# A new order for the opening of an encoder step, with a third pair of projections run ahead

## The chip, the cores and the metric

The kernel runs on one core of a Trainium2 chip. The metric is the time of one execution on the device in microseconds (us); less is better. The engines are named as the profile names them: PE is TensorE's matmul, PEld its weight load, DVE VectorE, ACT ScalarE, POOL GpSimd, and SP SyncE, whose queue issues nearly all transfers.

## The reference

One layer of a streaming encoder works on 1024 prompt positions and 8 times 16 sample positions, 1152 rows (T) in all, in float32.

```python
h = rmsnorm(x, g_pre_mix)
qa, ka, va, qb, kb, vb, ga, gb = split(h @ w_in)          # 34 tiles of 128 columns
oa = band_attention(qa, ka, va, t5 bias, sink)             # 2 chunks back
ob = band_attention(qb, kb, vb, relative bias)             # 8 chunks back
x = x + rmsnorm((sigmoid(ga) * (oa @ w_oa) + sigmoid(gb) * (ob @ w_ob)) @ w_out, g_post_mix)
u, g = split(rmsnorm(x, g_pre_ffn) @ w_upg)
x = x + rmsnorm((gelu(causal_conv3(u)) * g) @ w_down, g_post_ffn)
```

It returns x and the new key, value and convolution rows. Only the first two lines and the two bias tables bear on this change.

## The kernel before

**Stage.** Everything that changes lies in the kernel's first stage: h is made and multiplied by `w_in`. Each float32 operand is kept as two float32r parts, a high one (a rounded copy that ACT makes) and a low one (the rest, that DVE makes by a subtraction), and a product takes three matmuls, high by high, low by high, high by low.

**Pairs and the seven products.** Two 128-column tiles of `w_in` form a pair (`pairs`, line 199; twelve of them). The 1024 features and the 1152 rows are each cut in two, and a pair is computed by a scheme of seven block products in place of eight, on sums and differences of blocks. The right factors are b11, b21 (first 576 rows, two halves of the features), b12, b22 (last 576 rows) and four sums t1 to t4. The 576 rows of a half are done in two chunks of 256 and 320 columns, so a block product is 24 matmuls (`product`, `chunk_product`, lines 137 to 148).

**What is run ahead.** Two of a pair's products, a11 by b11 and a12 by b21, need only the first 576 rows and no sums. For the first `NA` = 7 pairs they are done before everything else by the class `Away` (line 234): it splits two weight tiles into parts (`ih`, line 176 ACT and 177 DVE), `run(i, c)` does 12 matmuls of product i on chunk c (`ixh`), and `copy(i, c)` takes the running sum out of PSUM (`ia0h`, `ia1h`, line 251); run(1, c) adds to the same bank and so waits for copy(0, c). The results are stored (lines 253, 255) and loaded again later (`ia`, line 483).

**The opening.** The 1152 rows come as nine blocks of 128 (`xt`). A block goes through five steps: `enter` (ACT squares and sums, line 296, then DVE line 96 and POOL line 97 make the inverse root), `norm` (DVE, line 306, or 303 for blocks 0 and 1), `transposed` (PE, eight transposes into two PSUM banks, line 314), `high` (ACT copies out of PSUM, line 330) and `low` (DVE, line 335; only the rows of b11 and b21, blocks 0 to 3 and half of 4). Chunk 0 of b11 and b21 is blocks 0 and 1; chunk 1 is blocks 2, 3 and half of 4. Blocks 4 (second half) to 8 fill b12 and b22. A list written by hand (lines 345 to 405) gives the order of these steps and of the Away steps of pairs 0 and 1 on ACT, DVE and PE; each of these engines takes what it is given strictly in order. Pair 2's Away comes behind the list, then those of pairs 3 to 6 (line 511).

**The tables of biases.** In the opening the two tables are made (`eb`, lines 410 to 415; `ea`, lines 417 to 424, by one small matmul `pe`), stored to DRAM (`tab_b`, `tab_a`) and spread there by `replicate` (line 87) to 128 copies for each of eight heads: `ext_b` and `ext_a`, eight transfers each on SP. The attention stage reads them from about 287 us on.

**The tails.** `right_factors` (line 429) makes t3, t2, t1, the parts of b22, t4 and the parts of b12, one step for each `next(forms)`. Then `tail` (line 486) does the pairs one after the other: for a pair that was run ahead five products (t3 into `iz`, then t2, t1, b22 into `ix`, then t4 into `iz`), 120 matmuls. Between them `take` (line 487, DVE line 191) adds the stored part `ia` to the running sum, before PE may add the next product to the same bank. Weights come by `weights(f)` (line 217, two transfers `iw`, two buffers shared with those of Away), the left sums by `left_factors` (lines 127 to 133). Tail 0 is that of pair 0, and so on.

**What sets the order elsewhere.** Behind the list a scheduler orders each engine's instructions at build time: those written first go first among those that it believes ready. SP's queue is one line in that order. `issue_after(x)` puts what it holds behind x on x's own engine.

Of the kernel before, what the change touches and what calls it, by code (L numbers as in the profile page):

```python
# [14 lines left out]
ALU = mybir.AluOpType  # L15
# [37 lines left out]
def encoder_step(ctx, tc, x, w_in, w_o, w_out, w_upg, w_down, kc, vc, state_conv, conv_w, conv_b,  # L53
# [30 lines left out]
        return [[(r1[2 * g + i] if g < 2 else r2).tile([P, KD, GW], F32R, name=f"{name}{g}{'hl'[i]}", tag="act")  # L84
                 for i in range(2)] for g in range(NG)]

    def replicate(tab, ext, sb, n):

        nc.sync.dma_start(tab[:], sb[:])
        t = tab[:]  # L90
        for h in range(8):
            nc.sync.dma_start(ext[h], bass.AP(tensor=t.tensor, offset=t.offset + h * n, ap=[[0, P], [1, n]]))
# [57 lines left out]
    def banks(pool, name, widths=(CW, CW)):  # L150
        return [pool.tile([P, 512], F32, name=f"{name}_{c}", tag="ps")[:, 0:n] for c, n in enumerate(widths)]
# [6 lines left out]
    def chunk(c):  # L158
        return slice(c * widths[0], widths[0] + c * widths[1])
# [3 lines left out]
    with ExitStack() as ph:  # L163
# [7 lines left out]

        b12, b22 = [rq.tile([P, 4, 2 * CW], F32, name=n) for n in ("b12", "b22")]

        def split_left(src, name):
            sp = wop.tile([P, 2, 4, P], F32R, name=name, tag="wop")
            nc.scalar.activation(sp[:, 0], src, AF.Copy)  # L176
            nc.vector.tensor_tensor(sp[:, 1], src, fr(sp[:, 0]), op=ALU.subtract)
            return sp

        def two_chunks(name):  # L180
            return pa.tile([P, 2 * CW], F32, name=name, tag="a")

        def copy_out(ps, t):
            for c in range(2):
# [3 lines left out]
        def plus(ps, t, out=None):  # L188
# [2 lines left out]
                nc.vector.tensor_tensor(out[:, chunk(c)], ps[c], t[:, chunk(c)], op=ALU.add)  # L191
            return out

        def store(t, tile_no, half):
            nc.sync.dma_start(in_dr[tile_no][:, half * 2 * CW:(half + 1) * 2 * CW], t[:])

# [15 lines left out]
        def weights(f):  # L214
            raw = wraw.tile([P, 2, KD, P], F32, name=f"iw{f}", tag="uw")
            for i in range(2):
                nc.sync.dma_start(raw[:, i], w_in[pairs[f][i]])
            return raw
# [15 lines left out]
        class Away:  # L234


            def __init__(self, f, pool, early=False):
                self.f, self.pool, self.early = f, pool, early
                raw = away_weights(f)
                self.left = [split_left(raw[:, 4 * i:4 * i + 4], f"ih1{i}_{f}") for i in range(2)]  # L240
                self.out = [two_chunks(f"ia{i}h{f}") for i in range(2)]
                self.ps = [None, None]

            def run(self, i, c):
# [19 lines left out]
        with ExitStack() as pre:  # L264
# [70 lines left out]
                            nc.vector.tensor_tensor(xk[q][:, 1, :, t], pt[:, :, c], fr(xk[q][:, 0, :, t]),  # L335
                                                    op=ALU.subtract)

            b = []

            def enter():  # L340
                b.append(Block(len(b)))
                b[-1].square()

            with tc.manual_schedule(engines={mybir.EngineType.Activation, mybir.EngineType.DVE, mybir.EngineType.PE}):
                enter()
                b[0].norm()
                enter()
                b[0].transposed()
                for i in range(2):
                    nc.scalar.activation(gp[:, i * 512:(i + 1) * 512], gps[i][:], AF.Copy)  # L350
                b[1].norm()
                b[0].high()
                b[0].low()
                w0 = Away(0, psx, True)
                b[1].transposed()
                b[1].high()
                b[1].low()
                enter()
                w0.run(0, 0)
                b[2].norm()  # L360
                w0.copy(0, 0)
                w1 = Away(1, psx, True)
                enter()
                b[2].transposed()
                b[2].high()
                w0.run(1, 0)
                b[2].low()
                b[3].norm()
                w0.copy(1, 0)
                enter()  # L370
                w1.run(0, 0)
                b[3].transposed()
                b[3].high()
                b[4].norm()
                w1.copy(0, 0)
                b[3].low()
                w1.run(1, 0)
                b[4].transposed()
                b[4].high()
                b[4].low()  # L380
                w1.copy(1, 0)
                enter()
                b[5].norm()
                w0.run(0, 1)
                w0.copy(0, 1)
                enter()
                w1.run(0, 1)
                b[5].transposed()
                b[5].high()
                w1.copy(0, 1)  # L390
                b[6].norm()
                w0.run(1, 1)
                enter()
                w0.copy(1, 1)
                b[6].transposed()
                b[6].high()
                b[7].norm()
                w1.run(1, 1)
                enter()
                w1.copy(1, 1)  # L400
                b[7].transposed()
                b[7].high()
                b[8].norm()
                b[8].transposed()
                b[8].high()

            Away(2, psx).all()


            rr = xs.tile([8, 2 * CLIP + 1], F32, name="rr")  # L410
# [2 lines left out]
            nc.vector.memset(eb[:, 0:512], 0.0)  # L413
            nc.vector.tensor_scalar(eb[:, 0:512], eb[:, 0:512], rr[:, 0:1], -1.0, op0=ALU.add, op1=ALU.mult)
            nc.vector.tensor_scalar(eb[:, 512:EXT_B], rr[:, 0:EXT_B - 512], -1.0, None, op0=ALU.mult)
            replicate(tab_b, ext_b, eb, EXT_B)
            tt = xs.tile([T5_BUCKETS, 8], F32, name="tt")
            oh = xs.tile([T5_BUCKETS, EXT_A], F32, name="oh")
            nc.sync.dma_start(tt[:], t5t)
# [2 lines left out]
            nc.tensor.matmul(pe[0:8, 0:EXT_A], tt[:], oh[:], start=True, stop=True)  # L422
            ea = xs.tile([8, EXT_A], F32, name="ea")
            nc.scalar.activation(ea[:], pe[0:8, 0:EXT_A], AF.Copy, scale=-1.0)
            replicate(tab_a, ext_a, ea, EXT_A)

        tpool = [ph.enter_context(tc.tile_pool(name=f"t{i}", bufs=1, reuse_waits="tile")) for i in (3, 2, 1, 4)]

        def right_factors():

            for n, pool in zip(("t3", "t2", "t1"), tpool):
                rf[n] = pool.tile([P, 2, 4, 2 * CW], F32R, name=n)
            sums = tpool[3].tile([P, 2, 4, 2 * CW], F32, name="sums", tag="t")
            t3 = t2 = sums[:, 0]
            t1 = sums[:, 1]

            def sub(c, out, a, b):
                nc.vector.tensor_tensor(*[t[:, :, chunk(c)] for t in (out, a, b)], op=ALU.subtract)

            def part(name, i):  # L440
                return fr(rf[name][:, i])

            for c in range(2):
                sub(c, t3, b22, b12)
                parts_of(rf["t3"], c, t3)
            yield
            for c in range(2):
                sub(c, t1, b12, part("b11", 0))
                sub(c, t1, t1, part("b11", 1))
                sub(c, t2, b22, t1)  # L450
                parts_of(rf["t2"], c, t2)
            yield
            for c in range(2):
                parts_of(rf["t1"], c, t1)
            yield
            for c in range(2):
                parts_of(rf["b22"], c, b22)
            yield
            for c in range(2):
                sub(c, b22, part("b21", 0), t2)  # L460
                nc.vector.tensor_tensor(*[t[:, :, chunk(c)] for t in (b22, b22, part("b21", 1))], op=ALU.add)
            rf["t4"] = tpool[3].tile([P, 2, 4, 2 * CW], F32R, name="t4", tag="t")
            for c in range(2):
                parts_of(rf["t4"], c, b22)
            yield
            for c in range(2):
                parts_of(rf["b12"], c, b12)
            yield
# [12 lines left out]
        def head_back(f):  # L481
            a = two_chunks(f"ia{f}")
            nc.sync.dma_start(a[:], a1_dr[f][:])
            return left_factors(weights(f), True, f"i{f}", split_left), banks(psx, f"ix{f}", widths), a

        def tail(f, ops, xb, a, forms):
            def take(name):
                t = two_chunks(f"{name}{f}")
                return copy_out(xb, t) if a is None else plus(xb, a, t)

            t0, t1 = pairs[f]
            zb = banks(psz, f"iz{f}", widths)
            product(zb, next(ops), of(rf["t3"]), True, False)
            next(forms, None)
            product(xb, next(ops), of(rf["t2"]), a is not None, False)
            next(forms, None)
            u2 = take("iu")
            product(xb, next(ops), of(rf["t1"]), False, False)
            next(forms, None)
            u4 = take("iv")  # L500
            store(plus(zb, u4), t1, 1)
            product(xb, next(ops), of(rf["b22"]), False, True)
            next(forms, None)
            store(take("iw"), t0, 1)
            product(zb, next(ops), of(rf["t4"]), False, True)
            store(plus(zb, u2), t1, 0)
            next(forms, None)

        forms = right_factors()
        next(forms)  # L510
        for f in range(3, NA):
            Away(f, psz if f % 2 else psx).all()
        for f in range(len(pairs)):
            tail(f, *(head_back(f) if f < NA else head(f)), forms)


    wr = wr_stack.enter_context(tc.tile_pool(name="wr", bufs=2, side="right", reuse_waits="tile"))
# [1187 lines left out]
```

## Time and profile before

| | |
|---|---|
| time, median of 3 runs | 1612.9 us (1612.63 to 1615.28) |
| the profiled execution's own time | 1616.09 us |
| its span in the trace | 1614.3 us |
| PE busy | 1587.8 us (98%) |
| DVE busy | 1106.3 us (69%) |
| ACT busy | 727.7 us (45%) |
| granted clock of PE | 0.997 of full speed |

The profiled execution took 1.8 us more than its span, which is what lies around the traced instructions. Matmuls overlap, and their ends are modelled, so PE counts as busy also where it runs thin: in the opening the number of matmuls done in a stretch tells more than the busy time. In rows of the timeline the first number is the start, the second the length of the whole row; the time in brackets is how long the engine had been idle before it, and the name behind the arrow what ended that. A wait on several things is put down to the last one by the profile, which can name an engine that had long been done.

### The profile page before, as it was taken

The page shows a single profiled execution, that of the slowest core. Times are in us where ns is not written, and L with a number is a line of the kernel's source. Part 1 is how long each engine was busy: PE and PEld are TensorE (multiplying, and loading weights), DVE is VectorE, ACT ScalarE, POOL GpSimd, SP SyncE. Part 2 cuts the span into 40 slices and gives each one's busy share as a digit, 9 for nine tenths or more (in the row PEclk, how much of TensorE's full clock was granted, in tenths as well). Part 3 has the DMA queues.
Part 4 walks back from the last instruction along what each step waited for, and adds up shares of the span by engine and source line. Part 5 has one row for each costly group of instructions (what it writes and reads, how often), then busy time and mean ns, then how long its engine had stood idle before and what let it go on. Part 6 is the DMA issues. An engine that isn't in the chain of part 4 may idle for free.

```text
span 1614.3 us, 27934 instructions
## 1 busy us (share of the span) xinstructions
PE 1587.8 (98%) x10891; PEld 1467.1 (91%) x10891; DVE 1106.3 (69%) x2055; ACT 727.7 (45%) x1428; POOL 212.5 (13%) x287
## 2 busy tenths in 40 slices
PE   8999999999999999999999999999999999999998
PEld 7999999878788789988899999999999998888886
DVE  6976534677777765453498777667666677956987
ACT  7621233666555554332374444444444445434353
POOL 1000000221110004410002221122111211000002
PEclk9999999999999999999999999999999999999999
DMA  7654321754543164452253333212222128063023
GB/s 274 219 185 147 110 96 75 228 177 145 165 151 128 63 219 155 126 184 97 73 172 107 112 97 97 77 62 82 74 77 79 59 75 347 1 223 110 1 83 152
DMA packets 93045, 205.94 MB, mean 128 GB/s; under 512 B 19321, under 2 KB 42793, under 8 KB 92914
## 3 DMA queue, kind: packets, MB, share of 16 engines
q1 hardware_dynamic: 92640, 203.35, 36.7%
q8 instruction: 85, 1.39, 0.4%
q0 software_dynamic: 272, 0.81, 0.1%
q14 instruction: 46, 0.38, 0.1%
q10 hardware_dynamic: 2, 0.00, 0.0%
HBM read 147.61 MB, written 61.24 MB: 129 GB/s over the span
## 4 chain that ended last, share of the span: by engine, by line
PE 87%; DVE 4%; DMA 2%; ACT 2%; issue 1%; SPq 0%; DVEq 0%; POOLq 0%; ACTq 0%
PE x L143 18%; PE z L143 10%; PE x L1487 8%; PE ix L143 7%; PE p L1487 6%; PE iz L143 4%; PE y L143 4%; PE o L754 2%; PE d L117 2%; PE d L119 2%; PE pt L739 2%; PE d L118 2%; PE xh L143 2%; PE mp L965 2%; PE mp L967 2%; PE mp L966 2%
## 5 line engine op out<-in xcount | busy, mean ns | idle before, releaser
L143 PE MATMUL x<-xot,s 128*128 128x288 f32 x1152 | 157.7, 295 | 0.0
L143 PEld LDWEIGHTS x<-xot,s 128*128 128x128 f32 x1152 | 155.0, 188 | 0.1
L1487 PE MATMUL x<-wbp,zap 128*128 128x512 f32 x576 | 135.3, 389 | 0.0
L1487 PEld LDWEIGHTS x<-wbp,zap 128*128 128x128 f32 x576 | 108.1, 188 | 22.4
L705 ACT ACTIVATE p<-p,m 128x256 f32<-128x256 f32 (+4 forms) x128 | 74.8, 586 | 59.1 <-DVE m L700 59.0
L1487 PE MATMUL p<-wbp,zap 128*128 128x512 f32 x432 | 100.7, 389 | 0.1
L1088 ACT ACTIVATE s<-uw 128x512 fp32r<-128x512 f32 x96 | 60.2, 628 | 85.2 <-PE z L143 38.3
L1487 PEld LDWEIGHTS p<-wbp,zap 128*128 128x128 f32 x432 | 81.0, 188 | 17.3 <-ACT yacc L1497 0.5
L1292 DVE SCALAR_TENSOR_TENSOR wk<-w,cw,wk 128x448 f32<-128x448 f32 (+1 forms) x144 | 88.0, 651 | 2.8 <-ACT wk L1290 1.9
L1089 DVE TENSOR_TENSOR s<-uw,s 128x512 fp32r<-128x512 f32 x96 | 67.9, 708 | 31.1 <-ACT s L1088 30.7
L1089 DVE TENSOR_TENSOR a<-uw,a 128x512 fp32r<-128x512 f32 x62 | 42.8, 691 | 58.4 <-ACT a L1088 57.4
L143 PE MATMUL z<-xot,a 128*128 128x288 f32 x576 | 80.8, 295 | 0.0
L143 PE MATMUL x<-xob,s 128*128 128x288 f32 x576 | 80.8, 295 | 0.0
L143 PE MATMUL z<-xot,s 128*128 128x288 f32 x576 | 80.7, 295 | 0.0
L143 PEld LDWEIGHTS x<-xob,s 128*128 128x128 f32 x576 | 78.1, 188 | 0.1
L143 PEld LDWEIGHTS z<-xot,a 128*128 128x128 f32 x576 | 78.2, 188 | 0.0
L143 PE MATMUL ix<-t,s_i 128*128 128x256 f32 (+1 forms) x576 | 78.1, 294 | 0.0
L143 PEld LDWEIGHTS z<-xot,s 128*128 128x128 f32 x576 | 78.1, 188 | 0.0
L143 PEld LDWEIGHTS ix<-t,s_i 128*128 128x128 f32 x576 | 76.7, 188 | 0.0
L176 ACT ACTIVATE s_i<-iw 128x512 fp32r<-128x512 f32 x48 | 30.1, 631 | 83.8 <-PE ix L143 38.1
L143 PE MATMUL x<-xob,a 128*128 128x288 f32 x456 | 64.0, 295 | 0.0
L143 PE MATMUL y<-xob,a 128*128 128x288 f32 x456 | 64.0, 295 | 0.0
(638 smaller groups left out, 3832.6 us busy)
## 6 DMA issues: line engine op xcount, KB each, us to landing
uw<-in_w_upg SPq DMA_DIRECT2D x53, 512.0 KB, 3.8
iw<-in_w_in SPq DMA_DIRECT2D x24, 512.0 KB, 3.8
gg<-in_dr SPq DMA_DIRECT2D x16, 576.0 KB, 3.8
z_dr<-wk SPq DMA_DIRECT2D x23, 256.0 KB, 2.1
in_dr<-gt SPq DMA_DIRECT2D x30, 192.0 KB, 1.9
z_dr<-wk SPq DMA_DIRECT2D x23, 224.0 KB, 1.9
xt<-in_x SPq DMA_DIRECT2D x9, 512.0 KB, 7.8
oT<-o_dr SPq DMA_DIRECT2D x8, 576.0 KB, 4.3
```

What stands on the lines that cost most here:

```text
L117: nc.tensor.matmul(ps, w[:, 0, a], xg[0][:, b], start=start and k == 0, stop=False)
L118: nc.tensor.matmul(ps, w[:, 0, a], xg[1][:, b], start=False, stop=False)
L119: nc.tensor.matmul(ps, w[:, 1, a], xg[0][:, b], start=False, stop=stop and k == nk - 1)
L143: nc.tensor.matmul(ps, w[:, i, k], right(j, c, k), start=first and n == 0, stop=last and n == len(todo) - 1, skip_group_check=True)
L705: nc.scalar.activation(p[h][:, 0:n], p[h][:, 0:n], AF.Exp, bias=least[h], scale=-1.0, accum_out=st.d[:, h, i:i + 1])
L739: nc.tensor.transpose(pt[:, h * nb + b], st.p[i][h][:, c:c + P], ident[:])
L754: nc.tensor.matmul(ps[r, c], k.vs[:, kb, r], p[h], start=n == 0, stop=n == len(st.pv) - 1)
L965: nc.tensor.matmul(ps[:], self.sp[:, 0, k], oT[k][:, 0, c], start=k % 4 == 0, stop=False)
L1088: split["left"] = nc.scalar.activation(sp[:, 0], src, AF.Copy)
L1089: split["low"] = nc.vector.tensor_tensor(sp[:, 1], src, fr(sp[:, 0]), op=ALU.subtract)
L1292: nc.vector.scalar_tensor_tensor(out, src(t), cw[:, f, t:t + 1], out, op0=ALU.mult, op1=ALU.add)
L1487: nc.tensor.matmul(ps, z[:, i, k, c], w[:, j, k], start=first and n == 0, stop=last and n == 2, skip_group_check=True)
```

## The change

1. The list of the opening is written as a string of steps in another order. Pair 2's Away (`w.2`, `run.2.*`, `cp.2.*`) is now in the list, with its parts and outputs in pools of its own (`wop3`, `pa3`). `w.0` comes ahead of `transposed.0`, and block 8 and 7 come ahead of 5 and 6.
2. `replicate` keeps only the sixteen spreading transfers, and these are issued behind the last store of tail 2. The two small stores to `tab_b` and `tab_a` stay where they were.
3. The pools of t1 to t4 are opened in another order, 4 first, so that the scratch tile `sums` lies elsewhere in memory.
4. Tail 0 makes t2 before its own first left sum, which is put behind the last of t2's subtractions on DVE.
5. The weights of pairs 4 and 6 (for Away) are asked for with those of pair 3, and pair 0's full weights before Away 5 is run.

```diff
-    def replicate(tab, ext, sb, n):
-        nc.sync.dma_start(tab[:], sb[:])
+    def replicate(tab, ext, n):
...
-            with tc.manual_schedule(engines={...}):
-                enter()
-                b[0].norm()
-                enter()
-                b[0].transposed()
...
-            Away(2, psx).all()
+            wop3, pa3 = [pre.enter_context(tc.tile_pool(name=n, bufs=2)) for n in ("wop3", "pa3")]
+            def weights_of(f):
+                w[f] = Away(f, psx, True, wop if f < 2 else wop3, pa if f < 2 else pa3)
...
+                written = """
+                    enter.0 norm.0 enter.1 w.0 transposed.0 gp norm.1 high.0 transposed.1 low.0 enter.2 high.1 low.1
+                    run.0.0.0 norm.2 enter.3 w.1 norm.3 run.1.0.0 cp.0.0.0 enter.4 transposed.2 w.2 high.2 low.2
+                    transposed.3 run.2.0.0 norm.4 enter.8 run.0.1.0 high.3 cp.1.0.0 transposed.4 low.3 norm.8
+                    enter.7 high.4 low.4 cp.0.1.0 norm.7 run.1.1.0 transposed.8 enter.5 enter.6 norm.5 norm.6 high.8
+                    cp.1.1.0 run.0.0.1 transposed.7 cp.2.0.0 run.2.0.1 transposed.5 high.7 transposed.6 high.5
+                    run.1.0.1 high.6 run.2.1.0 cp.0.0.1 cp.1.0.1 run.0.1.1 run.1.1.1 cp.2.0.1 cp.1.1.1 run.2.1.1
+                    cp.2.1.0 cp.0.1.1 cp.2.1.1
+                """
...
-            replicate(tab_b, ext_b, eb, EXT_B)
+            nc.sync.dma_start(tab_b[:], eb[:])
...
-            replicate(tab_a, ext_a, ea, EXT_A)
+            nc.sync.dma_start(tab_a[:], ea[:])
...
-        tpool = [... for i in (3, 2, 1, 4)]
+        tpool = {i: ... for i in (4, 3, 2, 1)}
...
-            return left_factors(weights(f), True, f"i{f}", split_left), banks(psx, f"ix{f}", widths), a
+            raw = raws.pop(f, None) or weights(f)
+            return left_factors(raw, True, f"i{f}", split_left), banks(psx, f"ix{f}", widths), a
...
-            product(zb, next(ops), of(rf["t3"]), True, False)
-            next(forms, None)
+            if f:
+                first = next(ops)
+            else:
+                next(forms)
+                with tc.issue_after(rf["sub"].ins):
+                    first = next(ops)
+            product(zb, first, of(rf["t3"]), True, False)
...
         for f in range(3, NA):
-            Away(f, psz if f % 2 else psx).all()
+            e = Away(f, psz if f % 2 else psx)
+            if f == 3:
+                away_weights(4)
+                away_weights(6)
+            if f == 5:
+                raws[0] = weights(0)
+            e.all()
         for f in range(len(pairs)):
             tail(f, *(head_back(f) if f < NA else head(f)), forms)
+            if f == 2:
+                with tc.issue_after(held["store"].ins):
+                    replicate(tab_b, ext_b, EXT_B)
+                    replicate(tab_a, ext_a, EXT_A)
```

In the list `run.f.i.c` is run(i, c) of pair f, `cp.f.i.c` its copy, `w.f` the making of its parts, and the number behind the other names is the block.

## Rows read from the trace of the kernel before

**Rows 1.** The page, its first part (busy time of each engine with its share of the span and its instructions) and the head of its fourth (the chain of work that ended last, by engine).

```profile
PE 1587.8 (98%) x10891; PEld 1467.1 (91%) x10891; DVE 1106.3 (69%) x2055; ACT 727.7 (45%) x1428; POOL 212.5 (13%) x287
...
PE 87%; DVE 4%; DMA 2%; ACT 2%; issue 1%; SPq 0%; DVEq 0%; POOLq 0%; ACTq 0%
```

**Rows 2.** The timeline of PE, from the first product to the third tail: start, length, what, count of matmuls, idle before.

```profile
11.47 3.06 PE L143 MATMUL ixh<-xk,ih 128*128 128x256 f32 x12
...
24.40 1.04 PE L314 MATMUL tp<-ident,xn 128*128 128x128 f32 x8
...
44.33 0.81 PE L422 MATMUL pe<-oh,tt 32*8 32x384 f32 x2
45.06 15.11 PE L143 MATMUL ixh<-xk,ih 128*128 128x256 f32 x113
...
68.27 3.44 PE L143 MATMUL ixh<-xk,ih 128*128 128x256 f32 x24 [0.73 <-ACT ia0h L251]
71.55 3.33 PE L143 MATMUL iz<-t,s_i 128*128 128x256 f32 x24
...
85.98 2.92 PE L143 MATMUL iz<-t,a_i 128*128 128x256 f32 x20 [0.91 <-DVE a_i L177]
88.74 3.33 PE L143 MATMUL iz<-t,s_i 128*128 128x256 f32 x24
...
104.60 3.33 PE L143 MATMUL iz<-t,s_i 128*128 128x256 f32 x24
```

**Rows 3.** The stretches 20 to 30, 30 to 40 and 70 to 80 us: length, then busy time and count of PE, PEld, DVE, ACT, POOL, then granted clock, DMA share, GB/s.

```profile
20.00:30.00 10.00, 8.31 (x62) 7.61 (x61) 5.79 (x12) 7.37 (x18) 1.14 (x3) 1.00 0.40 127
30.00:40.00 10.00, 9.44 (x73) 9.02 (x74) 6.57 (x9) 8.82 (x19) 1.60 (x3) 1.00 0.86 264
70.00:80.00 10.00, 10.00 (x77) 10.00 (x76) 10.00 (x13) 4.39 (x7) 0.00 (x0) 1.00 0.20 67
```

**Rows 4.** The chain of waits through tail 0: start, length, what.

```profile
71.72 0.67 DVE s_i L177
...
85.33 0.61 DVE a_i L177
```

**Rows 5.** The timeline of DVE between the end of the opening's list and the first subtraction of t3.

```profile
40.42 1.23 DVE L212 TENSOR_TENSOR xk<-b,xk 128x1024 fp32r<-128x1024 f32 x1 [1.67 <-ACT xk L211]
...
48.55 2.63 DVE L438 TENSOR_TENSOR sums<-b,b 128x1024 f32<-128x1024 f32 x2 [1.37 <-PE ixh L143]
```

**Rows 6.** The timeline of SP's queue, the storing and spreading of the small table.

```profile
45.81 0.29 SPq L89 DMA_DIRECT2D tab_a<-ea  x1
...
48.44 4.97 SPq L92 DMA_DIRECT2D ext_a<-tab_a  x8
```

**Rows 7.** The timeline of ACT in the opening.

```profile
5.70 1.06 ACT L296 ACTIVATE xn<-xt 128x1024 f32<-128x1024 f32 x1
...
7.21 1.25 ACT L350 ACTIVATE gp<-gps 128x512 f32<-128x512 f32 x2 [0.36 <-DVE xn L303]
...
14.57 0.38 ACT L251 ACTIVATE ia0h<-ixh 128x256 f32<-128x256 f32 x1 [1.57 <-PE ixh L143]
14.86 1.14 ACT L176 ACTIVATE ih<-iwh 128x512 fp32r<-128x512 f32 x2
15.90 1.04 ACT L296 ACTIVATE xn<-xt 128x1024 f32<-128x1024 f32 x1
...
16.94 0.58 ACT L330 ACTIVATE xk<-tp 128x512 fp32r<-128x512 f32 x1
```

**Rows 8.** The timeline of DVE in the opening: norm of block 4, low of block 3.

```profile
21.96 1.28 DVE L306 SCALAR_TENSOR_TENSOR xn<-xt,st,gp 128x1024 f32<-128x1024 f32 x1 [0.73 <-POOL st L97]
23.16 1.28 DVE L335 TENSOR_TENSOR xk<-tp,xk 128x512 fp32r<-128x512 f32 x2
```

**Rows 9.** The view of transfers, for those issued between 1.64 and 2.1 us and between 10.76 and 11.35 us: count, KB each, median time from issue to landing.

```profile
iwh<-in_w_in SPq DMA_DIRECT2D x1, 512.0 KB, 5.9
...
iwh<-in_w_in SPq DMA_DIRECT2D x2, 512.0 KB, 9.7
```

**Rows 10.** The timeline of SP's queue where pair 2's and pair 3's weights for Away are asked for.

```profile
10.38 0.90 SPq L225 DMA_DIRECT2D iwh<-in_w_in  x2
```

**Rows 11.** The stretches 28 to 36, 34 to 36 and 36 to 48 us, columns as in Rows 3.

```profile
28.00:36.00 8.00, 7.36 (x55) 6.89 (x54) 5.43 (x8) 7.49 (x16) 1.85 (x4) 1.00 0.78 236
34.00:36.00 2.00, 2.00 (x16) 1.77 (x15) 1.36 (x2) 2.00 (x5) 0.32 (x1) 1.00 0.76 200
36.00:48.00 12.00, 11.44 (x84) 10.43 (x83) 9.03 (x9) 9.93 (x18) 0.23 (x1) 1.00 0.90 307
```

**Rows 12.** The view of transfers of the first 330 us: count, KB each, median time from issue to landing.

```profile
ext_b<-tab_b SPq DMA_DIRECT2D x8, 384.0 KB, 6.0
...
ext_a<-tab_a SPq DMA_DIRECT2D x8, 192.0 KB, 4.6
```

**Rows 13.** The timeline of SP's queue from the end of tail 2 into tail 3.

```profile
121.19 0.32 SPq L195 DMA_DIRECT2D in_dr<-iu  x1
125.29 0.81 SPq L217 DMA_DIRECT2D iw<-in_w_in  x2
126.19 0.38 SPq L483 DMA_DIRECT2D ia<-a_dr  x1
```

**Rows 14.** The timeline of DVE, first take of tail 2.

```profile
109.39 0.42 DVE L191 TENSOR_TENSOR iu<-ix,ia 128x256 f32<-128x256 f32 x1
```

More of the change, by code (lines that the diff above doesn't have):

```diff
@@ L172, in encoder_step, with split_left @@
         b12, b22 = [rq.tile([P, 4, 2 * CW], F32, name=n) for n in ("b12", "b22")]
-        def split_left(src, name):
-            sp = wop.tile([P, 2, 4, P], F32R, name=name, tag="wop")
+        def split_left(src, name, pool=wop):
+            sp = pool.tile([P, 2, 4, P], F32R, name=name, tag="wop")
             nc.scalar.activation(sp[:, 0], src, AF.Copy)
@@ L178, in split_left, with two_chunks @@
             return sp
-        def two_chunks(name):
-            return pa.tile([P, 2 * CW], F32, name=name, tag="a")
+        def two_chunks(name, pool=pa):
+            return pool.tile([P, 2 * CW], F32, name=name, tag="a")
         def copy_out(ps, t):
@@ L192, in plus @@
             return out
+        held = {}
         def store(t, tile_no, half):
-            nc.sync.dma_start(in_dr[tile_no][:, half * 2 * CW:(half + 1) * 2 * CW], t[:])
+            held["store"] = nc.sync.dma_start(in_dr[tile_no][:, half * 2 * CW:(half + 1) * 2 * CW], t[:])
         pairs = [(4, 5), (0, 1), (2, 3), (10, 14), (6, 7), (11, 15)] + [(18 + n, 26 + n) for n in range(6)]
@@ L234, in encoder_step, with __init__ @@
         class Away:
-            def __init__(self, f, pool, early=False):
+            def __init__(self, f, pool, early=False, wop=wop, pa=pa):
                 self.f, self.pool, self.early = f, pool, early
                 raw = away_weights(f)
-                self.left = [split_left(raw[:, 4 * i:4 * i + 4], f"ih1{i}_{f}") for i in range(2)]
-                self.out = [two_chunks(f"ia{i}h{f}") for i in range(2)]
+                self.left = [split_left(raw[:, 4 * i:4 * i + 4], f"ih1{i}_{f}", wop) for i in range(2)]
+                self.out = [two_chunks(f"ia{i}h{f}", pa) for i in range(2)]
                 self.ps = [None, None]
@@ L336, in low @@
                                                     op=ALU.subtract)
[L338 to L344, printed above, removed]
-                enter()
-                b[0].norm()
-                enter()
-                b[0].transposed()
+            wop3, pa3 = [pre.enter_context(tc.tile_pool(name=n, bufs=2)) for n in ("wop3", "pa3")]
@@ L349, in encoder_step, with enter, spread_weights @@
+            b, w = {}, {}
+            def enter(tb):
+                b[tb] = Block(tb)
+                b[tb].square()
+            def weights_of(f):
+                w[f] = Away(f, psx, True, wop if f < 2 else wop3, pa if f < 2 else pa3)
+            def spread_weights():
                 for i in range(2):
                     nc.scalar.activation(gp[:, i * 512:(i + 1) * 512], gps[i][:], AF.Copy)
[L351 to L405, printed above, removed]
@@ L407, in encoder_step @@
-            Away(2, psx).all()
+            steps = dict(enter=enter, gp=spread_weights, w=weights_of,
+                         run=lambda f, i, c: w[f].run(i, c), cp=lambda f, i, c: w[f].copy(i, c))
+            for name in ("norm", "transposed", "high", "low"):
+                steps[name] = lambda tb, name=name: getattr(b[tb], name)()
+            with tc.manual_schedule(engines={mybir.EngineType.Activation, mybir.EngineType.DVE, mybir.EngineType.PE}):
+                written = """
[7 more added lines that the diff above has]
+                """
+                for step in written.split():
+                    name, *args = step.split(".")
+                    steps[name](*map(int, args))
@@ L424, in encoder_step @@
             nc.scalar.activation(ea[:], pe[0:8, 0:EXT_A], AF.Copy, scale=-1.0)
-            replicate(tab_a, ext_a, ea, EXT_A)
-        tpool = [ph.enter_context(tc.tile_pool(name=f"t{i}", bufs=1, reuse_waits="tile")) for i in (3, 2, 1, 4)]
+            nc.sync.dma_start(tab_a[:], ea[:])
+        tpool = {i: ph.enter_context(tc.tile_pool(name=f"t{i}", bufs=1, reuse_waits="tile")) for i in (4, 3, 2, 1)}
         def right_factors():
-            for n, pool in zip(("t3", "t2", "t1"), tpool):
-                rf[n] = pool.tile([P, 2, 4, 2 * CW], F32R, name=n)
-            sums = tpool[3].tile([P, 2, 4, 2 * CW], F32, name="sums", tag="t")
+            sums = tpool[4].tile([P, 2, 4, 2 * CW], F32, name="sums", tag="t")
+            for i in (3, 2, 1):
+                rf[f"t{i}"] = tpool[i].tile([P, 2, 4, 2 * CW], F32R, name=f"t{i}")
             t3 = t2 = sums[:, 0]
@@ L437, in sub @@
             def sub(c, out, a, b):
-                nc.vector.tensor_tensor(*[t[:, :, chunk(c)] for t in (out, a, b)], op=ALU.subtract)
+                rf["sub"] = nc.vector.tensor_tensor(*[t[:, :, chunk(c)] for t in (out, a, b)], op=ALU.subtract)
             def part(name, i):
@@ L461, in right_factors @@
                 nc.vector.tensor_tensor(*[t[:, :, chunk(c)] for t in (b22, b22, part("b21", 1))], op=ALU.add)
-            rf["t4"] = tpool[3].tile([P, 2, 4, 2 * CW], F32R, name="t4", tag="t")
+            rf["t4"] = tpool[4].tile([P, 2, 4, 2 * CW], F32R, name="t4", tag="t")
             for c in range(2):
@@ L507, in tail @@
             next(forms, None)
+        raws = {}
         forms = right_factors()
```

## The prediction, made before the changed kernel had run

> **What bounds the kernel now.** I read the page's busy times first, then the stretches of the first 90 us, then PE's timeline there, the chain of waits, and last SP's queue and the transfers. The page says that PE is the bound: 98% busy and 87% of the chain that ended last [rows 1]. A change to the opening can therefore win only what PE loses there. The timeline shows what that is. Tail 1 takes 104.60 − 88.74 = 15.86 us for 120 matmuls, so 48 of them, one pair's Away, need 6.35 us when nothing holds PE up, a run on chunk 0 (256 columns) 1.41 us and one on chunk 1 (320 columns) 1.76 us, if the 3.17 us of one block product are shared out by columns. The first product starts at 11.47, the small matmul `pe` at 44.33 ends the Aways of pairs 0 to 2, those of pairs 3 to 6 fill 45.06 to 71.55, and tail 0 ends at 88.74 [rows 2].
>
> Three losses lie in this. From 45.06 to 71.55 are 26.5 us for 25.4 us of work: 1.1 lost, 0.73 of it while PE waited for a copy of ACT. Tail 0 takes 17.2 us for 15.9: 1.3 lost, 0.91 of it in front of its last product [rows 2]. There DVE is the bound: it is busy in every tenth of 70 to 80 us [rows 3], and the chain of waits runs through DVE from 71.72 until the last left part is done at 85.94 [rows 4]. And the opening is thin: 62 and 73 matmuls in 20 to 30 and 30 to 40 us against 77 in 70 to 80 [rows 3]. Nothing behind 88.74 stands in PE's way until the attention stage, so I take it that what is won by then is won at the end.
>
> **Part by part.** *The list.* I lay the new order out on ACT, which takes its steps one by one. A step of `enter` costs 1.04 us (15.90 to 16.94), a pair's two weight parts 1.04 (14.86 to 15.90), a copy of 256 columns 0.29 (14.57 to 14.86), the two `gp` copies 1.25, and `high` I take as 1.04 like the weight parts, of the same size [rows 7]. Block 1's square ends at 6.85 [rows 7]. Pair 0's weights are asked for at 1.64 and land 5.9 later [rows 9], so w.0 runs 7.55 to 8.6; gp to 9.85, high.0 to 10.9, enter.2 to 11.9, high.1 to 12.95, enter.3 to 14.0, w.1 to 15.05, the first copy to 15.35, enter.4 to 16.4. w.0 ahead of norm.1 puts its two subtractions in DVE's way, and the first product starts near 12.5 and no longer at 11.47. Next on ACT is w.2, and its weights are not there: SP asks for pair 2's and pair 3's from 10.38 on [rows 10], behind nine blocks, and the one landing shown took 9.7 us [rows 9]. I read it as the second, near 20.5, and the first 512 KB earlier, near 19.2. So ACT stands still for 2.8 us, with high.2, enter.8 and high.3 queued behind it, and DVE and PE behind these.
>
> The Trainium skill says that ACT and DVE are strict first-in first-out queues (TensorE: Matmul & The Clock Gate, its section on the 16 sub-arrays). The trace agrees: a copy kept ACT idle for 1.57 us in front of weight parts that come behind it [rows 7]. If ACT could pass over w.2, the sum below would gain 2.4 us more.
>
> From there the chain is w.2 to 20.25, its low parts on DVE and low.2 (1.20 a pair, 21.96 to 23.16 for a step of this size [rows 8]) to 22.3, norm.4 (1.20) to 23.5. Behind transposed.4 PE has something to do at every step: five transposes of about 1.0 (the one at 24.40 [rows 2]), two runs on chunk 0 and six on chunk 1 = 5.0 + 2.8 + 10.6, with `pe` (0.73) 19.1. I add 0.3 for small waits: the Aways of pairs 0 to 2 end at 42.9 against 45.06, 2.2 us won.
>
> *Pairs 3 to 6 and tail 0.* DVE's long chain starts at 48.55 before, and not because of PE, which the row names: `sums` lay where the small table was, whose store was issued at 45.81 and had landed by 48.44, when the spreading began [rows 5, 6]. With the pools in the other order that wait is gone, and DVE may start when the last `high` is done. ACT, put on through the list, reaches that near 34.5. DVE needed at most 85.9 − 40.4 = 45.5 us from the parts of b12 to the last left part, 1.4 of it idle [rows 4, 5]; with pair 3's parts (1.2) that is 45.3 us, or 79.8. PE asks for the last product at 42.9 + 25.4 + 12.7 = 81.0. So DVE is no longer late, by a little over 1 us, and I count both later losses as gone: 42.9 + 25.4 + 15.9 = 84.2 against 88.74, **4.5 us** won. If they stay (1.1 + 1.3), 2.1 is left.
>
> *Weights asked for sooner, t2 ahead of the first left sum, the new pools.* I take 0. The buffers are still two, so a request waits for the split that frees one, whenever it is written; the first left sum loses nothing on DVE, which starts its long chain 14 us earlier (34.5 against 48.55), while PE is only 2.2 earlier. Bounds: the losses just named, 2.4 either way. `wop3` and `pa3` lie where t1 comes, long after pair 2 is done.
>
> *The spreading.* It leaves the opening, where its share of DMA (0.90 of 36 to 48 us [rows 11]) held up nothing that PE waited for; this saves 0, at most 2.8 if pair 2's weights gained from it, which lie earlier. It comes behind the store at 121.19, in front of pair 5's weights (125.29) and tail 4's `ia` (126.19) [rows 13]. SP needs 0.6 us an issue (8 in 4.97 [rows 6]), 9.6 us for 16, and the stores of tail 3 wait in the same line. Ahead of `ia`'s end then lie 8 × 384 + 8 × 192 KB [rows 12], 1024 KB of weights and its own 288 KB: 6.06 MB. The stretch of 36 to 48 us, full of such transfers, moved 307 GB/s, that of 28 to 36 moved 236 [rows 11]: 19.7 or 25.7 us from 121.8, so 141.5 or 147.5. `ia` is wanted in tail 4: its first take would be at 104.60 + 2 × 15.86 + 4.79 = 141.1 [rows 2, 14], and as PE works on chunk 1 for 1.76 us meanwhile, and DVE takes 0.42 + some 0.2, PE is held from about 142.2. Behind that take wait the rest of DVE's line, so the next parts too. Cost: 0 to 5.3 us; I take **0.5**, near the fuller stretch. The weights, wanted near 147, have room.
>
> The Trainium skill gives some 358 GB/s as one core's limit on HBM (DMA: Bandwidth & Descriptors, its section on bandwidth); by that estimate the burst takes 16.9 us and costs 0. The rows show less than that in each stretch with spreading in it.
>
> **Sum.** −4.5 + 0.5 = −4.0. The profiled execution took 1616.1 (span 1614.3 and 1.8 around it), which would be 1612.1; it lies 3.2 above the median of 1612.9, which becomes **1608.9 us**.
>
> **The rivals.** *More than that:* if SP asks for pair 2's weights ahead of the last blocks, ACT doesn't stand still; of its 2.8 us DVE keeps 0.4, whose own line behind w.1 and norm.3 reaches norm.4 no earlier than 21.1, so the chain is 2.4 earlier and the sum is 1606.5. For it: the request depends on nothing. Against: before, it came behind all nine blocks [rows 10].
>
> *No change that counts:* the opening wins its 2.2 us, but ACT and DVE stand in each other's way as before in pairs 3 to 6 and tail 0 (2.4 stays), and the burst costs 0.5 or more: 1611.2. For it: DVE's margin is only about 1 us, and ACT takes copies for PE in the same line as work that waits for DVE.
>
> *Slower:* the burst drains slowly. One stretch in its midst (34 to 36) moved 200 GB/s [rows 11]; at that rate `ia` lands at 121.8 + 30.3 = 152.1, tail 4 stands 9.9 us, and against 4.5 won the time is 1612.9 + 5.4 = 1618.3. It turns slower than before under 243 GB/s (4.5 us of standing), and by more than 0.2% under 213. Against: in the slow stretches SP was spacing the issues, with stores in between that waited for ACT.
>
> *The change doesn't do what it says* would show as transfers of `ext_b` still in the opening, and belongs with no change.
>
> **How the numbers follow.** Forecast 0.43, more 0.15, no change 0.29, slower 0.13. A measurement here tells 0.2%, 3.2 us, from no change: faster 0.58, same 0.29, slower 0.13. The forecast's own range is 1606.5 to 1609.7. The whole range reaches on both sides: 1604 (both bounds of the opening, no cost of the burst) to 1614.5 (2.1 won, 3.7 lost), leaving out most of slower.
>
> **What would show it.** Right: ACT idle some 2 to 3 us in front of w.2's parts near 16 to 19; `pe` or the first run of pair 3 near 42 to 43; the first subtraction of t3 near 35; tail 0 starting near 68.3, with no wait in front of its last product, and ending near 84; tails of 15.9 us after it, but for tail 4, up to 1 us longer. Wrong: no such idle time of ACT and tail 0 ended by 82; or DVE still full until tail 0's last product; or tail 4 (or 3) stretched by 3 us and more, with DVE waiting for `ia`; or a stage behind 282 us longer by what the opening won.

## The result, and the profile after

Eleven executions of the changed kernel took 1623.6 us in the median (1614.9 to 1626.3), eleven of the kernel before, beside them, 1616.7 (1612.6 to 1619.0). The ratio is 1.0031, interval 1.0017 to 1.0046: slower by 0.31%, some 5 us, where 0.25% faster was forecast. (Ratios here are those on record, with their 95% intervals; they are not the quotients of the medians beside them.) The profiled execution took 1618.2 us (span 1616.5, granted clock 0.996), 2.1 more than that of before. The page of after, its first part and the head of its chain, as in [rows 1]:

```profile
PE 1590.4 (98%) x10891; PEld 1467.3 (91%) x10891; DVE 1101.0 (68%) x2055; ACT 726.9 (45%) x1428; POOL 212.6 (13%) x287
...
PE 91%; DMA 4%; DVE 2%; ACT 2%; issue 1%; SPq 0%; POOL 0%; DVEq 0%; POOLq 0%; ACTq 0%
```

The bound is the same; the chain's share of DMA rose from 2% to 4%, and DVE's fell from 4% to 2%. The opening did what was forecast. ACT's timeline of after, at the parts of pair 2:

```profile
18.57 1.15 ACT L175 ACTIVATE ih<-iwh 128x512 fp32r<-128x512 f32 x2 [2.73 <-DMA iwh<-in_w_in]
```

PE's timeline of after: the opening's end, tail 0 (from 67.33), tail 4 (from 130.80), the end of the last tail and the first scores of the attention stage:

```profile
41.10 0.81 PE L386 MATMUL pe<-oh,tt 32*8 32x384 f32 x2
41.84 25.65 PE L142 MATMUL ixh<-xk,ih 128*128 128x256 f32 x192
67.33 3.33 PE L142 MATMUL iz<-t,s_i 128*128 128x256 f32 x24
...
83.20 3.33 PE L142 MATMUL iz<-t,s_i 128*128 128x256 f32 x24
...
130.80 3.33 PE L142 MATMUL iz<-t,s_i 128*128 128x256 f32 x24
133.97 3.33 PE L142 MATMUL ix<-t,s_i 128*128 128x256 f32 x24
140.06 4.78 PE L142 MATMUL ix<-t,s_i 128*128 128x256 f32 x24 [2.76 <-DVE iu L190]
...
151.03 3.33 PE L142 MATMUL iz<-t,s_i 128*128 128x256 f32 x24
...
293.83 0.34 PE L116 MATMUL d<-xk,w12s 128*128 128x384 f32 x1
...
301.26 0.50 PE L679 MATMUL s<-kah,q0h 64*128 64x128 f32 x4 [0.32 <-ACT q0h L573]
```

Tail 0 ends at 83.20 against 88.74 [rows 2]: 5.5 us won. Tail 4 takes 151.03 − 130.80 = 20.2 us where an undisturbed tail takes 15.9: PE stands 2.76, and the 24 matmuls behind it take 4.78 where the same 24 took 3.33. When the last tail ends, little of the gain is left. The same marks of PE in the kernel before:

```profile
295.00 0.34 PE L117 MATMUL d<-xk,w12s 128*128 128x384 f32 x1
...
295.80 0.33 PE L697 MATMUL s<-kah,q0h 64*128 64x128 f32 x2
```

The tails end 1.2 us earlier than before, but the scores start 5.5 later. In between PE does matmuls `d` of a later step, so little idle time shows it. What released tail 4 stands on DVE, what was late for it on SP. First DVE of after, with the first subtraction of the sums at its head (48.55 in [rows 5]):

```profile
33.06 1.23 DVE L403 TENSOR_TENSOR sums<-b,xk 128x1024 f32<-128x1024 f32 x1 [1.45 <-ACT b L331]
...
139.49 0.82 DVE L190 TENSOR_TENSOR iu<-ix,ia 128x256 f32<-128x256 f32 x2 [3.90 <-DMA ia<-a_dr]
```

Then SP's queue of after, the burst and the first loads of the attention stage:

```profile
116.02 5.17 SPq L91 DMA_DIRECT2D ext_b<-tab_b  x8
121.46 10.81 SPq L91 DMA_DIRECT2D ext_a<-tab_a  x8
132.49 0.41 SPq L196 DMA_DIRECT2D in_dr<-iv  x1
...
134.14 0.43 SPq L448 DMA_DIRECT2D ia<-a_dr  x1
...
294.02 0.32 SPq L565 DMA_DIRECT2D karaw<-in_dr  x1
```

The sixteen issues held SP's line for 16 us, and `ia` stood behind them. The last row is the other surprise: `karaw`, the rows from which the first keys are made, is asked for at 294.02, when the last product ends. Before, it was asked for 11.5 us earlier:

```profile
282.50 0.32 SPq L583 DMA_DIRECT2D karaw<-in_dr  x1
```

The stretches 130 to 140 and 140 to 150 us of after (columns as in [rows 3]) show the clock behind the stall:

```profile
130.00:140.00 10.00, 7.31 (x55) 7.04 (x53) 2.38 (x5) 1.26 (x2) 0.00 (x0) 0.98 0.94 320
140.00:150.00 10.00, 9.94 (x66) 9.97 (x66) 7.17 (x16) 1.90 (x3) 0.00 (x0) 0.85 0.56 221
```

The four executions of after under 1619 us, the profiled one among them, have a mean granted clock of 0.996 to 0.998, the seven over 1620 one of 0.992 to 0.994.

### The profile page after: what moved, and what is told of

Read it like the earlier page. It is cut to its first block, busy times and chain, and to the rows that moved or that the text cites. A ratio compares the mean times of both kernels' runs of the same rounds, so it can differ in the third digit from the quotient of the medians.

```text
span 1616.5 us, 27928 instructions
## 1 busy us (share of the span) xinstructions
PE 1590.4 (98%) x10891; PEld 1467.3 (91%) x10891; DVE 1101.0 (68%) x2055; ACT 726.9 (45%) x1428; POOL 212.6 (13%) x287
## 4 chain that ended last, share of the span: by engine, by line
PE 91%; DMA 4%; DVE 2%; ACT 2%; issue 1%; SPq 0%; POOL 0%; DVEq 0%; POOLq 0%; ACTq 0%
PE x L142 18%; PE z L142 10%; PE x L1469 8%; PE ix L142 7%; PE p L1469 6%; PE iz L142 4%; PE y L142 4%; PE o L736 3%; PE ixh L142 2%; PE pt L721 2%; PE d L116 2%; PE s L679 2%; PE d L118 2%; PE xh L142 2%; PE d L117 2%; PE mp L947 2%
```

## The experiments

Three theories. **P**: the new order of the pools (edit 3) puts the attention stage's first raw rows where a tile lies that the last product still reads. **B**: the burst of sixteen transfers holds up `ia`. **R**, the rival of both: the opening is simply no gain in the end, and the medians differ by the granted clock, whatever these two places do. Ratios are to the kernel before, run on the same chip (its medians there 1616.7 and 1616.4).

| run | median us | ratio, interval | tail 0 ends | tail 4 takes | tails end | first scores behind that |
|---|---|---|---|---|---|---|
| before | 1616.7 | 1 | 88.74 | 15.9 | 295.00 | 0.8 |
| after | 1623.6 | 1.0031, 1.0017 to 1.0046 | 83.20 | 20.2 | 293.83 | 7.4 |
| e1 | 1615.1 | 0.9988, 0.9979 to 0.9997 | 84.36 | 20.0 | 295.65 | 0.8 |
| e2 | 1616.2 | 0.9994, 0.9984 to 1.0004 | 84.87 | 19.9 | 295.13 | 2.0 |
| e3 | 1616.0 | 0.9999, 0.9989 to 1.0010 | 84.66 | 15.9 | 290.93 | 8.4 |
| e4 | 1611.5 | 0.9969, 0.9959 to 0.9980 | 83.09 | 15.9 | 289.36 | 2.0 |
| e5 | 1619.8 | 1.0031, 1.0017 to 1.0045 | 87.64 | 15.9 | 293.91 | 8.2 |
| e6 | 1616.4 | 1.0006, 0.9997 to 1.0016 | 87.04 | 17.3 | 295.51 | 0.8 |
| e7 | 1617.3 | 1.0006, 0.9996 to 1.0016 | 87.57 | 15.9 | 293.84 | 2.0 |
| e8 | 1611.0 | 0.9965, 0.9952 to 0.9977 | 81.20 | 15.9 | 287.46 | 2.0 |

**e1 and e2: after, the pools in the old order, or with t4's second.**

```diff
-        tpool = {... for i in (4, 3, 2, 1)}
+        tpool = {... for i in (3, 2, 1, 4)}      # e1
+        tpool = {... for i in (3, 4, 2, 1)}      # e2
```

> The changed kernel with one part undone: the pools of t1 to t4 are opened in the order of the kernel before (3, 2, 1, 4). Theory P (the order of the pools: the attention stage's first load lies where t4 lay, so it waits for the last product of the last tail, 294.0 us in the changed kernel against 282.5 before): the load of ka comes 11 to 12 us ahead of the end of the last tail again, the first scores come about 1 us behind that end and not 7, and the time falls by some 4 to 5 us, to 0 to +1 us against the kernel before. The subtractions of t3 start later (after pair 2's last run, near 42), and tail 0 loses at most 2 us by it. Theory B (the burst of spreading alone is the loss): the time stays some 5 us above the kernel before, and tail 4 still takes 20 us. Rival R (the medians differ only by where PE's clock happens to fall): no shift of the first load matters, and the ratio goes with the granted clock of the runs.

> The changed kernel with the pools opened in the order 3, 4, 2, 1: the attention stage's raw rows lie where t3 lay, which its last product frees 12 us ahead of the end, and the scratch tile still lies clear of the small tables. P: the load of ka near 281 to 282 on the changed kernel's clock, first scores 1 to 3 us behind the end of the last tail (the parts of q lie where t4 lay), time 3 to 5 us below the changed kernel, and DVE's chain starts at 33 as in it, so tail 0 ends at 83 us. B: no gain. R: no gain beyond what the clock of the runs explains.

In both `karaw` is asked for near 283 again (283.15 and 282.63), and both are 0.4% faster than after. In e1 the sums start at 44.25, as they share the small table's place again; tail 0 waits 0.66 us in front of its last product, and tail 1 another 0.64 for DVE. In e2 they start at 34.69 and both tails wait for nothing; its tail 0 ends at 84.87 and not at 83, as `pe` came 1.6 us later than in after. The stall of tail 4 stays in both. P holds; B is untouched by it.

**e3: after, the spreading dealt out, one transfer of each table behind each of tails 2 to 9. e4: e2 and e3 together.**

```diff
-    def replicate(tab, ext, n):
+    def replicate(tab, ext, n, heads):
...
-        for h in range(8):
+        for h in heads:
...
-            if f == 2:
+            if 2 <= f < 10:
                 with tc.issue_after(held["store"].ins):
-                    replicate(tab_b, ext_b, EXT_B)
-                    replicate(tab_a, ext_a, EXT_A)
+                    replicate(tab_b, ext_b, EXT_B, [f - 2])
+                    replicate(tab_a, ext_a, EXT_A, [f - 2])
```

> The changed kernel with the sixteen spreading transfers dealt out two at a time behind tails 2 to 9 in place of all behind tail 2. B: tail 4 takes 15.9 us again in place of 20.2, no fall of the clock there, the last tail ends at about 289.5 us (5.5 ahead of the kernel before), and the time is 4.4 us below the changed kernel, near +0.5 us against the kernel before. P: the stage ends 4.4 earlier as well, but the attention stage still begins with its first load behind the last product, and some 4 to 5 us of what was won are lost there. R: the time follows the granted clock, which should be a little higher as one fall is gone.

> Both cures together (pools 3, 4, 2, 1, and the spreading dealt out behind tails 2 to 9). P and B together: tail 4 takes 15.9 us, the last tail ends near 289.5, the first scores come within 3 us of it, and the time is 4 to 5.5 us below the kernel before (ratio 0.9966 to 0.9975). If only one of them holds: within 1 us of the kernel before. R: no clear difference from the kernel before.

PE's timeline of e4, the rows that answer to those of after:

```profile
67.22 3.33 PE L142 MATMUL iz<-t,s_i 128*128 128x256 f32 x24
...
83.09 3.33 PE L142 MATMUL iz<-t,s_i 128*128 128x256 f32 x24
...
130.69 3.33 PE L142 MATMUL iz<-t,s_i 128*128 128x256 f32 x24
133.86 6.51 PE L142 MATMUL ix<-t,s_i 128*128 128x256 f32 x48
...
146.56 3.33 PE L142 MATMUL iz<-t,s_i 128*128 128x256 f32 x24
...
289.36 0.34 PE L116 MATMUL d<-xk,w12s 128*128 128x384 f32 x1
...
291.36 0.50 PE L679 MATMUL s<-kah,q0h 64*128 64x128 f32 x4
```

What tail 0 won (5.65) is still there when the tails end (5.64). With both causes gone the same opening makes the kernel 0.31% faster than before. Taking P away is worth 0.37% of before's time without B's cure (after to e2) and 0.30% with it (e3 to e4), taking B away 0.32% and 0.25%: the two add up within the intervals. R as the whole story falls: among the executions with a granted clock of 0.996 to 0.998, six of e4 took 1612.0 us in the mean and 54 of the kernel before 1616.4. Clock is a large part of after's 5 us all the same: its four executions at that level took 1617.1, 0.7 more than before.

**e5: before, with t4's pool opened first. e6: before, with the sixteen transfers behind tail 2.**

```diff
-        tpool = [... for i in (3, 2, 1, 4)]
+        tpool = {i: ... for i in (4, 3, 2, 1)}            # e5
+        tpool = [tpool[i] for i in (3, 2, 1, 4)]          # e5
...
-            replicate(tab_b, ext_b, eb, EXT_B)            # e6: the store stays,
+            nc.sync.dma_start(tab_b[:], eb[:])            # ext_b and ext_a behind tail 2
...
```

> The kernel before with one part of the change alone: the pools of t1 to t4 opened in the order 4, 3, 2, 1, all else as it was. P: the first load of the attention stage (ka) moves from 12.5 us ahead of the end of the last tail to its very end, first scores some 7 us behind the end and not 1, the time rises by 4 to 6 us unless the opening gives some of it back. In the opening the first subtraction of t3 no longer waits for the store of the small table (48.4 us) and comes near 40.5, so DVE is ahead and the 0.91 us in front of tail 0's last product go: at most 2 us won there. Net +2 to +5 us. R: no difference that the granted clock of the runs doesn't explain.

> The kernel before with another part alone: the sixteen spreading transfers issued behind the last store of tail 2, all else as it was. B: tail 4 stands 2 to 4 us in front of its second sum while DVE waits for the stored part, PE's clock falls behind that in some of the runs, +3 to +5 us there; in the opening the transfers are gone, but nothing of PE waited for them, so at most 1 us is won (the subtraction of t3 may come up to 2 us earlier). Net +2 to +5 us. The reading before the result (the burst costs 0.5): within 1 us of the kernel before.

e5 shows P alone. Its sums start at 37.42, 11 us earlier than before, and tail 0 ends only 1.1 earlier: PE waits 1.59 for ACT's copy in front of the last run of pair 6. SP's queue of e5 then has the late load,

```profile
294.10 0.32 SPq L584 DMA_DIRECT2D karaw<-in_dr  x1
```

and the kernel is 0.31% slower than before. e6 shows B in the old order. Its tail 0 ends 1.7 us earlier than before (1.2 of them lie ahead of `pe`, which e5, with the spreading in the opening, has too), and tail 4 loses 1.4. PE's timeline of e6 there:

```profile
143.11 3.41 PE L142 MATMUL ix<-t,s_i 128*128 128x256 f32 x24 [1.14 <-DVE iu L190]
```

The stall is shorter than after's, and the 24 matmuls behind it run at full pace. Tail 1 loses 0.8 as well, 0.56 of it a wait for DVE. So the 2 to 5 us that were expected of the burst by itself did not come: 1.0006 can't be told from no change.

**e7: after, pools as in e2, the spreading back in the opening, right behind the two small stores.**

```diff
             nc.sync.dma_start(tab_b[:], eb[:])
+            replicate(tab_b, ext_b, EXT_B)
...
             nc.sync.dma_start(tab_a[:], ea[:])
+            replicate(tab_a, ext_a, EXT_A)
...
-            if f == 2:
-                with tc.issue_after(held["store"].ins):
-                    replicate(tab_b, ext_b, EXT_B)
-                    replicate(tab_a, ext_a, EXT_A)
```

> The changed kernel with the pools 3, 4, 2, 1 and the sixteen spreading transfers back in the opening, right behind the stores of the small tables. If moving them out of the opening was needed for the win there: the burst now meets the stores and weights of pairs 3 to 6, the scratch tiles come free later, and tail 0 ends 1 to 3 us later than in the version with both cures (84 to 86 us). If it was not needed: tail 0 ends at 83 to 84.5 us as there, all tails take 15.9 us, and the time is the same as with both cures, 4 to 5 us below the kernel before.

Tail 0 ends at 87.57, 2.7 us behind e2's, and 0.37% of time lies between e7 and e4. SP's queue of e7:

```profile
53.26 4.97 SPq L91 DMA_DIRECT2D ext_a<-tab_a  x8
...
60.99 1.17 SPq L218 DMA_DIRECT2D iw<-in_w_in  x2
```

PE's timeline of e7, the start of tail 0:

```profile
70.46 0.50 PE L142 MATMUL iz<-t,s_i 128*128 128x256 f32 x2 [1.63 <-ACT s_i L175]
71.80 3.20 PE L142 MATMUL iz<-t,s_i 128*128 128x256 f32 x22 [0.84 <-DVE s_i L176]
```

Pair 0's full weights, asked for at 51.2 in after, come behind the spreading here, and the first left sum of tail 0 keeps PE 2.5 us. So the new opening needs the spreading out of its way.

**e8: e4, with blocks 8 and 7 loaded ahead of 5 and 6, and the weights of pairs 2 and 3 asked for behind blocks 4 and 6.**

```diff
-            for tb in range(NT):
+            for tb in (0, 1, 2, 3, 4, 8, 7, 5, 6):
...
-                if tb in (1, 3):
+                if tb == 4:
+                    box = wraw.tile([P, 2, KD, P], F32, name="iwh2", tag="uw")
+                if tb in (1, 3, 4, 6):
...
```

> The version with both cures, and the blocks loaded in the order in which the list enters them (0 to 4, 8, 7, 5, 6), with pair 2's weights asked for behind block 4 and pair 3's behind block 6. It takes away what ACT waits for in front of w.2 (2.7 us in the changed kernel). If that wait sets the end of the opening, as the prediction had it, the small matmul pe comes 2 to 2.6 us earlier (near 38.5 to 39) and tail 0 ends by that much earlier, the time is 2 us below the version with both cures (6 to 7.5 us below the kernel before). The rival is that the blocks 5 to 8 then come later and hold ACT at their enter steps: less than 1 us won.

ACT's timeline of e8, the parts of pairs 1 and 2:

```profile
13.47 1.14 ACT L175 ACTIVATE ih<-iwh 128x512 fp32r<-128x512 f32 x2
...
15.82 1.15 ACT L175 ACTIVATE ih<-iwh 128x512 fp32r<-128x512 f32 x2
```

ACT no longer stands still in front of pair 2's parts, `pe` starts at 39.01 and tail 0 ends 1.9 us ahead of e4's. In the median 0.5 us of this is seen, inside the intervals, where 2 were expected: e8 has the lowest median here, but its lead over e4 is not shown.

**e9 and e10: after, unaltered, for two more traces.**

> The changed kernel, unaltered, for a second trace. Seven of its eleven executions so far took over 1620 us with a mean granted clock of 0.992 to 0.994, and the one that was traced is not among them (1618.2 us, 0.996, some 6.5 us of clock lost at most, of which 130 to 150 and 410 to 430 us hold about 1.7 + 1.7). Theory that the clock goes with the two new places: an execution over 1620 us shows the granted clock fall behind PE's idle time in tail 4 (130 to 150 us) or in the attention stage (290 to 430 us) for longer than in the first trace, by 3 to 6 us of time in all, and the marks ahead of 130 us stay where they were. Rival, that it is the chip's own and anywhere: the clock is lower in stretches where PE never stood still, or falls at places that the kernel before has too (700 to 720, 1600).

> The changed kernel, unaltered, for a third trace, with the same two expectations as for the second: with seven of eleven executions over 1620 us, one of the two is likely to be such a one. If both are at 0.996 and above, where the lost clock lies stays open.

They took 1617.2 and 1614.8 us (clock 0.997 and 0.999; one execution of the kernel before, beside them on another chip than the other experiments, took 1613.3), so neither is one of the slower executions, and where those lose their clock stays open. What they do show is tail 4 with two lengths of the same stall. PE's timeline of e9:

```profile
140.04 4.93 PE L142 MATMUL ix<-t,s_i 128*128 128x256 f32 x24 [2.73 <-DVE iu L190]
```

Its stretch (columns as in [rows 3]):

```profile
140.00:150.00 10.00, 9.96 (x65) 10.00 (x66) 7.10 (x15) 1.90 (x3) 0.00 (x0) 0.83 0.54 213
```

PE's timeline of e10:

```profile
138.96 3.36 PE L142 MATMUL ix<-t,s_i 128*128 128x256 f32 x24 [1.36 <-DVE iu L190]
```

And its stretch:

```profile
140.00:150.00 10.00, 10.00 (x78) 10.00 (x78) 9.10 (x18) 2.42 (x4) 0.00 (x0) 1.00 0.49 194
```

After a stall of 2.73 us the granted clock fell and tail 4 took 20.4 us; after one of 1.36 it didn't, and tail 4 took 17.4.

## Why the prediction was wrong

**The opening: right.** ACT stood 2.73 us at w.2 (2.8 forecast); the first run of pair 3 came at 41.84 (42.9), tail 0 started at 67.33 (68.3) and ended at 83.20 (84.2). Pairs 3 to 6 and tail 0 run without a gap in the trace, as DVE starts its sums at 33.06 (near 35 forecast). The same order came out 1.6 us later in e2 and e3 (tail 0 from 68.96 and 68.80). The rival *more than that* was right in its mechanism: e8 did away with the wait and gained 1.9 us by tail 0, of 2.4 priced.

**"Nothing behind 88.74 stands in PE's way until the attention stage": the step that failed first.** It holds only as long as that stage's start stays where it was, and edit 3 moved it. I costed the pools' order by what lies under `sums` alone, and never asked what is put there next. `karaw`'s issue waits for the last product (before, it could go 12.5 us ahead of the tails' end), and the scores come 7.0 to 8.4 us behind the tails in after, e3, e5, e9 and e10, against 0.8 to 2.0 in the others. PE fills that time with `d`, yet most of it is lost later: in e3 and e10, whose clock stood at 1.00 from there to 710 us, the lead on before falls from 4.1 and 3.7 us at the tails' end to −0.8 at the first matmul of the later stage `r` (695.00 before, 695.83 in both). That mark alone doesn't single out P: in e4, without it, the lead falls from 5.6 to 1.6, but there the clock was 0.83 from 410 to 430 us. As an estimate, the missing share of the clock in those 20 us is 3.4 us in e4 and 1.8 in after. With such an estimate taken off in every trace, the way from the tails' end to the first `r` is 3.5 to 4.9 us longer than before in the five with the late load, and −1.0 to 1.5 in the other six. So P costs about 4 us there, and by the ratios 0.30 to 0.37%.

**The burst: sized wrong.** I took 0.5 us out of 0 to 5.3; tail 4 lost 4.4. The bytes were not far off: 4608 KB of tables, three stores and `ia`, 5.9 MB, from 116.02 to 139.49 is 251 GB/s, inside the 236 to 307 of [rows 11]. I took the fast end, because the fuller stretch moved more. But I had the issues wrong: the eight of `ext_a` took 10.81 us, where [rows 6] had 4.97 for the same eight, and `ia` was asked for only 18.1 us behind the first of the burst, where I had counted 9.6 us of issues. SP's queue of the kernel before had shown slow ones too, 1.1 us each:

```profile
36.60 4.34 SPq L92 DMA_DIRECT2D ext_b<-tab_b  x4
```

Whether the issues or the DMA engines set the pace of the burst is not shown: with the weights that were asked for behind `ia` counted in, 287 GB/s were moved in that time, at a DMA share of 0.91. The Trainium skill's limit of some 358 GB/s for one core (DMA: Bandwidth & Descriptors, its section on bandwidth), by which the burst cost nothing, was further from the measured 251 than my 307. I had also left out that a stall can cost more than its length: of the 4.4 us, 2.8 were idle and 1.6 clock (0.85). The rival *slower* named this mechanism, at a rate (200 GB/s) that did not come (its other bound, 213, should be about 215). By itself the burst does not make the kernel slower (e1, e2, e6). The whole range had room for 3.7 us of it, less than the 5.3 of its own sum.

**Leaving the opening: 0 taken, "at most 2.8".** e7 shows 2.7 us at tail 0 (against e2) for the new order, through the late request for pair 0's weights. I had read the 0 from the old order, where that request came at 55.8, some 2 us behind the end of the spreading, and PE did not wait for it. The change has the spreading out of the opening, so this is no part of the miss.

**The sum.** In the profiled executions 5.5 us were won by tail 0 and 4.4 lost in tail 4, which left 1.2 at the last tail's end; then P and a clock of 0.91 from 410 to 430 us put after 4.7 us behind before at the first `r`. Only 2.1 are left at the end; of what came back some 1.8, by the same estimate as above, is before's own clock, 0.91 from 700 to 720 us, where after's was 1.00. Two of the signs of being wrong had come: tail 4 stretched by more than 3 us with DVE waiting for `ia`, and the stage behind 282 us longer.

The rest of the 5 us lies in the seven executions at 0.992 to 0.994: after's median is 5.4 us above its profiled execution, that of before 0.6. Such executions, at 0.994 or less, go with the late load: 7 of 11 in after, 3 of 11 in e3, 3 of 12 in e5, and 3 of 122 in all the others together (one of the 61 of before that ran beside the experiments, two of e6, none of e1, e2, e4, e7 and e8). So part of what P costs in the ratios is clock; how the late load would bring it was not seen in a trace. Lastly, the three executions that the time before was read from were quick ones: 1612.9 became 1616.7 over eleven, so 1608.9 as a time was low by 3.8 us whatever the change did.

## What to carry to other kernels

When a change alters where tiles lie, list for each place what was there, what comes there, and what comes there next, up to the next stage: a load that starts when a buffer comes free moves with it, and a busy engine hides the loss. For a burst of transfers count how long it holds the queue that issues it, not its bytes alone: here 16 us, with a load behind them that PE came to wait for; dealt two to a tail the same transfers cost nothing that the traces show. A gain is only safe when the next stage's first load moves ahead with it: here 5.5 us at tail 0 became a slowdown, and 0.31% of gain once both were mended.

## What the runs showed of the hardware

Stalls of PE of 1.14 (e6) and 1.36 us (e10) left the granted clock at 1.00 in the stretch behind them; stalls of 2.23 to 2.76 us in the same place (after, e1, e2, e9) were followed by 0.83 to 0.85 from 140 to 150 us (in after 0.50, the lower level of 1.2 GHz, from 140 to 142), so a stall of twice the length cost tail 4 some three times as much (4.0 to 4.5 us against 1.4 to 1.5). It is not the length alone: PE idles 2.4 us somewhere between 407 and 418 us in every trace, and from 410 to 430 us the clock was 1.00 in before, e3 and e10, 0.91 in after, e2, e5, e6 and e9, and 0.83 in e1, e4, e7 and e8. What decides there stays open.
